# A hybrid RWKV/FNet/pooling trunk on one core: group matrices rebuilt in 64x64 quarters of the array, modulation products on four column strips

## The chip, the core and the metric

The kernel runs on one core of a Trainium2 chip. The metric is the device time of one execution in microseconds (us), as the median of several runs. The engines are TensorE (PE; its weight loads are listed as PEld), VectorE (DVE), ScalarE (ACT), GpSimd (POOL) and the DMA queues, of which SyncE (SP) issues most.

## What is computed

One layer of a trunk over 128 context tokens and 512 latent tokens of 1024 channels, all in float32:

```
shift1, scale1, gate1, shift2, scale2, gate2 = split(silu(cond) @ w_ada + b_ada)
h = rms_norm(x) * (1 + scale1) + shift1
proj = h @ w_in                        # columns for r, k, v, two low-rank inputs, FNet, pooling
y_a = rwkv_mixer(centred_shift(proj))  # 8 heads x 64, forward and backward
y_b = fourier_mixer(proj)              # y_c = pool_mixer(proj)
x = x + gate1 * (concat(y_a, y_b, y_c) @ w_out)
x = x + gate2 * (relu(h2 @ w_ff1)**2 @ w_ff2)      # h2 = modulated norm of x

# rwkv_mixer: decay and a come from low-rank products (w_up, a_up); then for each token
sa = S @ a;  S = S * w + sa b^T + v k^T;  y = S @ r
```

Outputs are the normed `x` of both token sets and the final state `S` of the context.

## The kernel before

**Products.** The large weights are split into two float32r parts (`whi`, `wlo`) and multiplied with the two parts of the activations, three products for each block: the tiles `hhi`/`hlo`, `mh`/`ml`, `h2h`/`h2l` and `fh`/`fl` are activations of w_in, w_out, w_ff1 and w_ff2. Small float32 products stand in the profile as two MATMUL records for each instruction, float16 ones and transposes as one.

**The mixer.** Time is cut into 10 chunks of 64 tokens; a head pair `j` (4 of them) and a direction `d` (2) have three groups of 2, 4 and 4 chunks, so there are 24 groups, 16 of four chunks and 8 of two. `prep` makes the elementwise operands of a group from two low-rank products (`wup` with `th`, `aup` with `adt`). `group` is a generator over stages, which yields after each: Gram blocks (`AR`,`BK`, result `EB`), the inverse of a triangular matrix of every chunk by doubling over five levels (`NB`, `X`, `XT`, `P1`) with one correction, the products W and Z, the matrices `OO`, and then a serial chain over the chunks that carries the state `x` (tiles `xr`) and adds to the output. Two 64-row blocks of a pair of chunks share the partitions. Before the change the operands `NB` and `XT` of the inverse (tiles `bda`) are block-diagonal, 128 x 128 with zero blocks; `oop` (tiles `oopa`) has zero blocks too; and `xr` has an identity in the half that the state doesn't use, so that one product with `OO` gives both terms.

**Order.** `run_groups` steps the generators of up to four groups while `Clock` estimates when each engine and tile is done. Where no group's next operands are there yet by that estimate, it steps the queue `gemms` (`in_rest`: the other w_in blocks; then the modulation of sections 2 to 5, `ada_steps`; then `out_half`: half of w_out), or, with that not ready, a dummy product on `lmask` whose result nobody reads. FNet, pooling and the transposes of x (`slow`), and `post` for each finished head pair (`y,bones`, `hsel,sq`, `ident,sq`, `kds,bones`, `sg,gup`) are stepped between. All engines issue in the order so traced.

**Modulation.** `ada_steps` multiplies the 32 columns of `sil` (two are used) with 512 columns of a 128-row block of `w_ada`; the four strips of 32 array columns belong to four row blocks, and in sections 2 to 5 each step brings one block.

After the mixer: the other half of w_out, the second norm, and the feed-forward product.

Of the kernel before, what the change touches and what calls it, by code (L numbers as in the profile page):

```python
# [13 lines left out]
F32 = mybir.dt.float32  # L14
# [146 lines left out]
class Clock:  # L161
    """estimate of when each engine and each tile is done with what has been traced; chooses what is traced next"""
# [7 lines left out]
    def __init__(self):  # L170
        self.free = dict.fromkeys("PVSGD", 0.0)
        self.done, self.used, self.slots = {}, {}, {}
        self.end = 0.0

    def cost(self, e, name, out, a, k):
        n = math.prod(out.shape[1:])
        if e == "P":
            if name == "transpose":
                return 55.0
            x = a[1]  # L180
            if x.dtype != F32:
                return n / 2.4 + (0.5 if x.dtype == F32R else 1.0)
            if out.shape[0] > 64:
                return max(211.0, n / 0.6 + 5.0)
            return 79.0 if n <= 64 else 133.0 * n / 128
# [10 lines left out]
    def tile(self, x):  # L196
        """name of the tile; a new one waits for the last use of the tile whose place it takes"""
# [12 lines left out]

    def note(self, e, name, out, a, k):
        rd = [self.tile(x) for x in list(a) + list(k.values()) if hasattr(x, "tensor")]
# [23 lines left out]
class Timed:  # L236
    """an engine whose instructions are noted on the clock"""
# [15 lines left out]
class Task:  # L253
# [4 lines left out]
    def step(self):  # L258
        """one step; it may yield the time that passes before the next, or the tile that the next reads first"""
# [11 lines left out]
def build(nc, tc, T):  # L271
# [10 lines left out]
    def pin(start):  # L282
        """the compute engines issue what was traced since start in the order of the program"""
# [35 lines left out]
    def wsplit(src, c0, hf, lo_eng, raw=None, to=None):  # L319
        """half of the rows of a block of 128 columns"""  # L320
# [9 lines left out]
    def gemm_steps(pss, w, a, kb, first, last, extra=0):  # L330
        """the products of one block of rows, as a generator over the matrix products"""
# [19 lines left out]
    def gemm(src, c0, a, lo_eng, halves=(0, 1), extra=0):  # L351
        """[P, NT] product with a block of 128 columns of the weights: two banks"""
# [32 lines left out]
    mod = cp.tile([P, 48, 2], F32, name="mod")  # L385

    def ada_steps(ks, slots, nk, ahead, queue=None):
        """sections of the modulation: 1024 columns each, 512 at a time; slots name the places of the weights"""
        todo = [(k, h, k2) for k in ks for h in range(2) for k2 in range(KB // nk)]
        place = {}  # L390

        def load(n):
            if queue is None and n < len(todo):
                k, h, k2 = todo[n]
                pool, tag, bufs = slots[n % len(slots)]
                place[n] = pool.tile([P, nk, 512], F32, tag=tag, name="wa", bufs=bufs)
                c0 = k * D + 512 * h
                dma(place[n][:], T["w_ada"][nk * k2 * P:nk * (k2 + 1) * P, c0:c0 + 512].rearrange("(a p) n -> p a n", p=P))

        for n in range(ahead):  # L400
            load(n)
        for n, (k, h, k2) in enumerate(todo):
            load(n + ahead)
            r = place.pop(n) if queue is None else queue.pop(0)
# [11 lines left out]
            yield  # L416
            ps2 = pm()
# [42 lines left out]
    XR = [[const(f"xr{d}{i}", [P, 2, C]) for i in range(3)] for d in range(2)]  # L460
# [24 lines left out]
    for d in range(2):  # L485
        for x in XR[d]:
            for q in range(2):
# [662 lines left out]
    def group(c, d, g, pool, own, pc, AR, BK):  # L1150
# [27 lines left out]
        if not M1:  # L1178
            yield
# [590 lines left out]
```

## Time and profile before

| | |
|---|---|
| median of 3 runs | 1140.12 us (1136.89 to 1140.99) |
| span of the profiled execution | 1140.2 us, which is its time |
| PE / PEld busy | 1095.3 us (96%) / 949.0 us (83%) |
| DVE / ACT / POOL busy | 544.5 / 506.4 / 383.3 us |
| mean granted TensorE clock | 0.983 of 2.4 GHz |

Busy PE is the union of the spans of pipelined products, so it doesn't tell how fast they follow each other. That is read from the start of a row of the timeline to the start of the next one, divided by the number of records in it.

### The profile page before, as it was taken

How to read it: one execution, taken by the hardware profiler on the slowest of the kernel's cores; microseconds unless marked ns; L12 is line 12 of the kernel's file. 1: busy time of each engine (PE TensorE's matmuls, PEld its weight loads, DVE VectorE, ACT ScalarE, POOL GpSimd, SP SyncE). 2: the span in 40 equal slices, each digit the busy share in tenths (PEclk: the TensorE clock that was granted, in tenths of full speed). 3: DMA queues.
4: the chain of work that ended last, by engine and by line, in shares of the span. 5: the costliest groups of instructions: out<-in, count | busy, mean ns of one | idle time of the engine just before them, and what ended most of it. 6: DMA issues, size and time to landing. Idle time of an engine off the chain costs nothing.

```text
span 1140.2 us, 23679 instructions
## 1 busy us (share of the span) xinstructions
PE 1095.3 (96%) x9516; PEld 949.0 (83%) x9516; DVE 544.5 (48%) x1297; ACT 506.4 (44%) x1221; POOL 383.3 (34%) x462
## 2 busy tenths in 40 slices
PE   5999999999999998998999999999999999999996
PEld 3688888788785665565677999999999999999996
DVE  6266665466665654667754664311331233123313
ACT  5243575655565454654762354312431243124412
POOL 4224431124222133464300283333333333333520
PEclk9999999999998999998999999999999999999999
DMA  9522311111313345442313322222222222222212
GB/s 321 184 62 81 94 36 58 51 51 43 95 64 121 112 139 166 124 133 69 111 56 97 117 74 75 75 75 75 75 76 80 76 76 75 75 74 75 77 45 93
DMA packets 130383, 104.11 MB, mean 91 GB/s; under 512 B 9309, under 2 KB 108642, under 8 KB 130274
## 3 DMA queue, kind: packets, MB, share of 16 engines
q1 hardware_dynamic: 114290, 81.22, 23.5%
q10 hardware_dynamic: 15552, 21.05, 6.2%
q8 instruction: 75, 1.23, 0.4%
q0 software_dynamic: 432, 0.33, 0.2%
q14 instruction: 34, 0.28, 0.1%
HBM read 90.52 MB, written 9.76 MB: 88 GB/s over the span
## 4 chain that ended last, share of the span: by engine, by line
PE 82%; issue 6%; DVE 6%; POOL 2%; ACT 1%; DMA 0%; ACTq 0%; DVEq 0%; POOLq 0%
PE pb L248 82%; DVE t L248 1%; DVE EB L248 1%; DVE bda L248 1%; POOL st L248 1%; DVE P L248 1%; DVE hlo L248 0%; DVE BK L248 0%; POOL t L248 0%; DMA wpl<-w_pool 0%; POOL bda L248 0%; ACTq L248 0%; DVE dd L248 0%; DVE W L248 0%; DVE y L248 0%
## 5 line engine op out<-in xcount | busy, mean ns | idle before, releaser
L248 POOL TENSOR_TENSOR wlo<-raw,whi 128x512 fp32r<-128x512 f32 x125 | 162.3, 1299 | 268.5 <-ACT whi L248 266.2
L248 ACT CAST whi<-raw 128x512 fp32r<-128x512 f32 x161 | 99.8, 620 | 276.6 <-PE pb L248 251.0
L248 PE MATMUL pb<-h2l,whi 128*128 128x320 f32 (+1 forms) x512 | 155.4, 310 | 0.0
L248 PE MATMUL pb<-h2h,whi 128*128 128x320 f32 (+1 forms) x512 | 155.3, 311 | 0.0
L248 DVE SCALAR_TENSOR_TENSOR x<-pb,mod,x 128x128 f32<-128x128 f32 (+1 forms) x144 | 55.0, 433 | 172.9 <-PE pb L248 172.7
L248 PE MATMUL pb<-fh,whi 128*128 128x320 f32 (+2 forms) x408 | 123.3, 310 | 0.0
L248 PE MATMUL pb<-fl,whi 128*128 128x320 f32 (+2 forms) x408 | 122.7, 308 | 0.0
L248 PE MATMUL pb<-h2h,wlo 128*128 128x320 f32 (+1 forms) x512 | 117.0, 310 | 0.0
L248 PE MATMUL pb<-hhi,whi 128*128 128x320 f32 (+1 forms) x304 | 99.1, 331 | 0.0
L248 PE MATMUL pb<-hlo,whi 128*128 128x320 f32 (+1 forms) x304 | 98.6, 329 | 0.4 <-DVE hlo L248 0.4
L248 PEld LDWEIGHTS pb<-h2l,whi 128*128 128x128 f32 x512 | 96.6, 189 | 0.0
L248 PEld LDWEIGHTS pb<-h2h,whi 128*128 128x128 f32 x512 | 96.5, 189 | 0.0
L248 PE MATMUL pb<-fh,wlo 128*128 128x320 f32 (+2 forms) x408 | 94.6, 309 | 0.0
L248 PEld LDWEIGHTS pb<-h2h,wlo 128*128 128x128 f32 x512 | 86.3, 188 | 0.0
L248 POOL TENSOR_TENSOR t<-t,k 128x256 f32<-128x256 f32 (+1 forms) x24 | 15.9, 664 | 208.2 <-DVE t L248 197.5
L248 PE MATMUL pb<-hhi,wlo 128*128 128x320 f32 (+1 forms) x304 | 78.8, 328 | 0.0
L248 PEld LDWEIGHTS pb<-fh,whi 128*128 128x128 f32 x408 | 77.1, 189 | 0.0
L248 PEld LDWEIGHTS pb<-fl,whi 128*128 128x128 f32 x408 | 76.3, 187 | 0.0
L248 DVE TENSOR_TENSOR rl<-pb,rs 128x320 f32<-128x320 f32 x64 | 30.3, 486 | 94.3 <-PE pb L248 94.1
L248 PEld LDWEIGHTS <-bda 128*128 128x128 f16 x880 | 43.1, 99 | 37.8 <-issue 13.9
L248 ACT COPY W<-pb 128x256 f32<-128x256 f32 (+3 forms) x144 | 54.4, 398 | 41.5 <-DVE W L248 29.2
L248 PEld LDWEIGHTS pb<-fh,wlo 128*128 128x128 f32 x408 | 68.6, 188 | 0.0
(271 smaller groups left out, 2399.7 us busy)
## 6 DMA issues: line engine op xcount, KB each, us to landing
raw<-w_ff SPq DMA_DIRECT2D x128, 256.0 KB, 2.8
wa<-w_ada SPq DMA_DIRECT2D x64, 256.0 KB, 3.2
wa<-w_ada SPq DMA_DIRECT2D x16, 512.0 KB, 8.7
raw<-w_in SPq DMA_DIRECT2D x30, 256.0 KB, 2.9
raw<-w_out SPq DMA_DIRECT2D x16, 256.0 KB, 2.8
ukd<-shq ACTq DMA_DIRECT2D x9, 320.0 KB, 2.5
ds<-dft_s ACTq DMA_DIRECT2D x8, 257.0 KB, 2.7
x<-x_sample SPq DMA_DIRECT2D x4, 512.0 KB, 5.8
```

Source lines behind the costliest of these rows:

```text
L248: return fn(out, *a, **k)
```

## The change

The operands with zero blocks go. The inverse is done with 64 x 64 products on the diagonal quarters of the array; `X` and `XT` share a tile `XX`, which leaves PSUM in one copy. The `OO` matrices come from 64 x 64 products `EB`,`WW` on all four quarters; the terms of Z and V go apart from them: `EB`,`ZV` gives `ZP`, which is added to the state in each chain step, and `ZV`,`EB` goes straight into the output bank. A chain step is one VectorE instruction on 128 partitions in place of one each on VectorE and ScalarE. The Gram products alternate between the two row halves. In `prep` the two low-rank products stand next to each other on opposite row halves (the two halves of the columns of that w_in block are swapped for it, so that its early load comes in two parts of 64 columns). `ada_quads` takes 128 columns of four row blocks in each step, on the four strips. The costs in `Clock` are new, among them one for every change of the shape of the array's tiles. Comments are removed as well.

```diff
--- before.py
+++ after.py
@@ class Clock
+            if x.dtype == F32R:
+                return n / 2.4 + 13.5
             if x.dtype != F32:
-                return n / 2.4 + (0.5 if x.dtype == F32R else 1.0)
-            if out.shape[0] > 64:
+                return n / 2.4 + 1.0 if x.shape[0] > 64 else 18.0
...
+    def mode(self, name, out, a):
+        m = (a[1].shape[0] > 64, out.shape[0] if name != "transpose" else P)
+        if m != self.was:
+            self.was = m
+            self.free["P"] += 95.0
@@ modulation
+    def ada_quads(ks, slots, ahead):
+        todo = [(k, h, cb, k2) for k in ks for h in range(2) for cb in range(4) for k2 in range(2)]
...
+                place[n] = pool.tile([P, 4, P], F32, tag=tag, name="wa", bufs=bufs)
...
+            for i in range(4):
+                q = 32 * i
+                mm(ps[q:q + 32, cb * P:(cb + 1) * P], sil[:, 4 * k2 + i, :], r[:, i, :], start=k2 == 0, stop=k2 == 1, tile_position=(0, q))
...
-        gemms.append(task(ada_steps((2, 4, 3, 5), [(wp, "whi", WB), (wp, "wlo", WB)], 1, AH)))
+        gemms.append(task(ada_quads((2, 4, 3, 5), [(wp, "whi", WB), (wp, "wlo", WB)], AH)))
@@ prep
-        ps = pm()
+        ps, ps2 = pm(), pm()
         mm(ps[:, 0:w], wup[rows, js], th[rows, cs], start=True, stop=True)
+        mm(ps2[:, 0:w], aup[HR[1 - d], js], adt[HR[1 - d], cs], start=True, stop=True)
...
-        mm(ps[:, 0:w], aup[rows, js], adt[rows, cs], start=True, stop=True)
@@ group: Gram blocks
+        pss = [pm(), pm()]
+        for l in range(n):
+            for h in range(2):
+                mm(pss[h][:, l * P:(l + 1) * P], BKc[HR[h], l * P:(l + 1) * P], AR[HR[h], :, l, :], start=True, stop=True)
@@ group: inverse
-            for u in range(U):
-                mm(ps[:, (o + u) * C:(o + u + 1) * C], lhs[:, u, :], rhs(u), start=True, stop=True)
+            for u, i, R in units():
+                mm(ps[R, (o + u) * C:(o + u + 1) * C], lhs[R, u, :], rhs(u, R), start=True, stop=True)
...
-            diag(XT, lambda u: p1[:, u, :])
-            for u, i, R in units():
-                mm(ps[R, (U + u) * C:(U + u + 1) * C], p1[R, u, :], XT[R, u, i * C:(i + 1) * C], start=True, stop=True)
+            diag(XT, lambda u, R: p1[R, u, :])
+            diag(p1, lambda u, R: XT[R, u, :], U)
...
-                cp(X[:, 0:U, :], v4(ps, C, U))
-                for i, R in enumerate(HR):
-                    cp(XT[R, 0:U, i * C:(i + 1) * C], ps[R, U * C:2 * U * C].rearrange("p (u b) -> p u b", b=C))
...
+                cp(XX[:, :, 0:U, :], both)
@@ group: O matrices
-        for h in range(2):
-            ps = pm()
-            for l in range(n):
-                mm(ps[:, l * P:(l + 1) * P], oop[:, l // 2, l % 2, h * P:(h + 1) * P], EB[:, h, l, C:3 * C], start=True, stop=True)
...
+        for l2 in range(n2):
+            for h in range(2):
+                for i in range(2):
+                    mm(pss[i][HR[h], l2 * P:(l2 + 1) * P], WW[HR[i], 2 * l2 + h, :], EB[HR[i], h, 2 * l2 + i, C:3 * C], start=True, stop=True)
...
+                mm(ps[HR[h], l * C:(l + 1) * C], EB[:, h, l, P:3 * C], ZV[:, l // 2, l % 2, h * C:(h + 1) * C], start=True, stop=True)
...
+        V.tensor_tensor(ZP[:, 0:n, :], v4(ps, C), pc[:, 0:n].unsqueeze(2).broadcast_to([P, n, C]), op=ALU.mult)
@@ group: chain
+                mm(psy[HR[h], l * C:(l + 1) * C], ZV[:, l // 2, l % 2, h * C:(h + 1) * C], EB[:, h, l, C:P], start=l == 0, stop=False)
...
-                    mm(ps[HR[q], 0:C], OO[:, q, l, C:P], x[:, q, :], start=True, stop=True)
+                    mm(ps[HR[q], 0:C], OO[HR[q], l, C:P], x[HR[q], :], start=True, stop=True)
...
-                V.tensor_scalar(xn[HR[0], 0, :], ps[HR[0], 0:C], pc[HR[0], l:l + 1], None, op0=ALU.mult)
-                S.activation(xn[HR[1], 1, :], ps[HR[1], 0:C], AF.Copy, scale=pc[HR[1], l:l + 1])
+                V.scalar_tensor_tensor(xn[:], ps[:, 0:C], pc[:, l:l + 1], ZP[:, l, :], op0=ALU.mult, op1=ALU.add)
```

What this makes of the program is seen in the order of the instructions, where `x8` is the number of equal ones in a row. PE in `prep` and the Gram blocks of an early group, before the change:

```order
L248 MATMUL pb<-th,wup 128x256
L248 MATMUL pb<-xr_109,W_1740 64x64 x2
L248 MATMUL pb<-W_1740,xr_109 64x64 x2
...
L248 MATMUL pb<-AR,BK 128x128 x8
L248 MATMUL pb<-adt,aup 128x256
L248 MATMUL pb<-ident,sq 128x128 x5
```

The two low-rank products stand apart, with a chain step and Gram products between. The same place after the change:

```order
L262 MATMUL pb<-hsel,sq 128x2 x4
L262 MATMUL pb<-th,wup 128x256
L262 MATMUL pb<-adt,aup 128x256
L262 MATMUL pb<-hsel,sq 128x2
L262 MATMUL pb<-EB,ZV 64x64 x4
L262 MATMUL pb<-xr_109,OO 64x64 x2
L262 MATMUL pb<-OO,xr_109 64x64 x2
```

The second low-rank product now follows the first at once; the chain step (`xr`,`OO`) has the same number of instructions.

PE at the end of the last group before the change, with its `OO` matrices (`EB`,`oopa`) and its first chain step; `mh`/`ml` with `whi`/`wlo` is `out_half`:

```order
L248 MATMUL pb<-W_8651 64x128 x8
L248 MATMUL pb<-mh,whi 128x320
...
L248 MATMUL pb<-ml,whi 128x320
L248 MATMUL pb<-EB,oopa_909 128x128 x8
L248 MATMUL pb<-mh,wlo 128x320 x2
...
L248 MATMUL pb<-xr_113,W_9114 64x64 x2
L248 MATMUL pb<-W_9114,xr_113 64x64 x2
```

And after the change, where `lmask` is the dummy:

```order
L262 MATMUL pb<-W_9437 64x128 x8
L262 MATMUL pb<-wa,sil 32x128 x4
...
L262 MATMUL pb<-EB,WW 64x128 x8
L262 MATMUL pb<-ZV,EB 64x64 x8
L262 MATMUL pb<-wa,sil 32x128 x4
L262 LDWEIGHTS lmask
L262 MATMUL pb<-lmask 128x512
...
L262 MATMUL pb<-EB,ZV 64x64 x8
L262 MATMUL pb<-xr_113,OO 64x64 x2
L262 MATMUL pb<-OO,xr_113 64x64 x2
```

Eight products of 128 x 128 became eight on quarters and two times eight on half the array's columns, and what stands between them is modulation (`wa`,`sil`) and dummies instead of w_out.

PE in `post` of the last head pair, before the change:

```order
L248 MATMUL pb<-y,bones 128x512
L248 MATMUL pb<-y,bones 128x128
L248 MATMUL pb<-ml,whi 128x320
L248 MATMUL pb<-mh,wlo 128x320 x2
L248 MATMUL pb<-hsel,sq 128x2
L248 MATMUL pb<-mh,whi 128x320
```

And after it:

```order
L262 MATMUL pb<-y,bones 128x512
L262 MATMUL pb<-y,bones 128x128
L262 MATMUL pb<-ident,xq 128x128 x8
L262 MATMUL pb<-mh,whi 128x320
L262 MATMUL pb<-hsel,sq 128x2
L262 MATMUL pb<-ml,whi 128x320
```

The first products of `out_half` stood far ahead of this place before the change; now the last transposes of x (`ident,xq`) and then the first of `out_half` are here. Of its 192 products, 111 stood ahead of the last `sg,gup` before, and 10 do now.

Counted over the whole program: the shape of PE's tiles (128 x 128, 64 x 64, 128 x 64, 64 x 128 or 128 x 32) changes 712 times before and 772 times after; dummies are 103 and 79; MATMUL instructions are 8093 and 9461. The 64 modulation steps of sections 2 to 5 stand in 36 places before and in 45 after (31 with one step, 10 with two, 3 with three, 1 with four).

## Rows read from the trace of the kernel before

**Rows 1.** Windows by stage: us, busy PE, PEld, DVE, ACT, POOL, PEclk, DMA share.

```profile
80.00:345.00 265.00, 261.77 (x2792) 217.04 (x2790) 168.63 (x423) 152.84 (x441) 77.69 (x136) 0.99 0.21 64
345.00:600.00 255.00, 237.87 (x2662) 159.27 (x2657) 155.56 (x405) 147.43 (x417) 84.56 (x122) 0.96 0.38 116
600.00:690.00 90.00, 86.46 (x623) 81.39 (x618) 51.59 (x106) 35.83 (x66) 35.65 (x25) 0.96 0.33 95
690.00:1140.20 450.20, 441.57 (x3009) 441.17 (x3007) 128.33 (x273) 140.36 (x237) 159.04 (x127) 1.00 0.25 74
```

**Rows 2.** Who PE waited for, 80 to 690 us: us, times, longest; 14 rows.

```profile
PE pb L248 <- DVE P L248: 4.2, 9, 1.5
...
PE pb L248 <- ACT y L248: 0.2, 1, 0.2
```

**Rows 3.** Timeline of PE (start, length us, records): inverse of a group.

```profile
136.99 0.22 PE L248 MATMUL pb<-X,bda 128*128 128x64 f16 x2
137.04 0.28 PE L248 MATMUL pb<-P,bda 128*128 128x64 f16 x4
137.25 0.31 PE L248 MATMUL pb<-bda,P 64*64 64x64 f16 x8
137.50 0.41 PE L248 MATMUL pb<-hhi,wlo 128*128 128x322 f32 x1
```

**Rows 4.** Timeline of PE: a modulation step of sections 2 to 5.

```profile
347.64 1.05 PE L248 MATMUL pb<-wa,sil 128*32 128x512 f32 x2
348.62 0.29 PE L248 MATMUL pb<-P,bda 128*128 128x64 f16 x4
```

**Rows 5.** Timeline of PE: products of 128 columns on four strips, first stage.

```profile
59.32 0.64 PE L248 MATMUL pb<-w,shp 128*32 128x128 f32 x16
59.89 0.41 PE L248 MATMUL pb<-hlo,whi 128*128 128x320 f32 x1
```

**Rows 6.** Timeline of PE: Gram products, four chunks and two.

```profile
160.67 1.71 PE L248 MATMUL pb<-AR,BK 64*128 64x128 f32 x16
...
228.47 0.72 PE L248 MATMUL pb<-AR,BK 64*128 64x128 f32 x8
```

**Rows 7.** Timeline of PE: the first of the two low-rank products.

```profile
139.43 0.70 PE L248 MATMUL pb<-th,wup 64*128 64x256 f32 x2
140.05 0.34 PE L248 MATMUL pb<-xr,W 128*64 128x64 f32 x4
```

**Rows 8.** Timeline of PE: O matrices of a group of four chunks.

```profile
609.57 1.95 PE L248 MATMUL pb<-EB,oopa 128*128 128x128 f32 x16
611.27 0.54 PE L248 MATMUL pb<-mh,wlo 128*128 128x320 f32 x2
```

**Rows 9.** Timeline of PE: five dummies and a chain step.

```profile
209.74 1.25 PE L248 MATMUL pb<-lmask 128*128 128x512 bf16 x5
210.92 0.34 PE L248 MATMUL pb<-xr,W 128*64 128x64 f32 x4
...
211.30 0.41 PE L248 MATMUL pb<-hhi,whi 128*128 128x320 f32 x1
```

**Rows 10.** Groups of ACT, 80 to 690 us: copies of the inverse, EB.

```profile
L248 ACT CAST bda<-pb 64x256 f16<-64x256 f32 x128 | 47.0, 368 | 1.0
L248 ACT CAST X<-pb 128x256 f16<-128x256 f32 x64 | 24.1, 377 | 16.6 <-PE pb L248 13.8 <-DMA oopa<-vt 1.8
L248 ACT COPY EB<-pb 128x512 f32<-128x512 f32 x16 | 9.4, 588 | 2.1 <-PE pb L248 1.7
```

**Rows 11.** Windows on both sides of a fall of PEclk.

```profile
273.00:276.40 3.40, 3.40 (x52) 2.99 (x50) 2.37 (x7) 1.79 (x6) 1.41 (x2) 1.00 0.04 12
276.40:279.80 3.40, 3.40 (x18) 3.34 (x19) 1.64 (x4) 2.61 (x10) 3.06 (x5) 0.50 0.05 10
```

**Rows 12.** Timeline of PE: post of the last head pair, its longest wait.

```profile
628.13 1.30 PE L248 MATMUL pb<-ident,sq 128*128 128x128 f32 x5 [1.94 <-DVE sq L248]
```

**Rows 13.** Who PE waited for, 0 to 80 us: modulation weights.

```profile
PE pb L248 <- DMA wa<-w_ada: 1.9, 2, 1.7
```

More of the change, by code (lines that the diff above doesn't have):

```diff
@@ L385, in build, with ada_steps @@
     mod = cp.tile([P, 48, 2], F32, name="mod")
-    def ada_steps(ks, slots, nk, ahead, queue=None):
+    def ada_steps(ks, nk, queue):
         todo = [(k, h, k2) for k in ks for h in range(2) for k2 in range(KB // nk)]
[L390 to L401, printed above, removed]
         for n, (k, h, k2) in enumerate(todo):
-            load(n + ahead)
-            r = place.pop(n) if queue is None else queue.pop(0)
+            r = queue.pop(0)
             yield r[:]
@@ L416, in ada_steps, with load @@
             yield
+            ps2 = pm()
+            for i in range(4):
+                PE.transpose(ps2[:, i * P:(i + 1) * P], asb[:, i * P:(i + 1) * P], ident[:])
+            ms = mod[:, 8 * k + 4 * h:8 * k + 4 * h + 4, :]
+            V.tensor_reduce(ms, ps2[:].rearrange("p (n q c) -> p n c q", n=4, q=4)[:, :, 0:2, :], axis=mybir.AxisListType.X, op=ALU.add)
+            V.tensor_tensor(ms, ms, pv("b_ada", 8 * k + 4 * h, 4).unsqueeze(2).broadcast_to([P, 4, 2]), op=ALU.add)
+            yield
+    def ada_quads(ks, slots, ahead):
+        todo = [(k, h, cb, k2) for k in ks for h in range(2) for cb in range(4) for k2 in range(2)]
+        place = {}
+        def load(n):
+            if n < len(todo):
+                k, h, cb, k2 = todo[n]
+                pool, tag, bufs = slots[n % len(slots)]
+                place[n] = pool.tile([P, 4, P], F32, tag=tag, name="wa", bufs=bufs)
+                c0 = k * D + 512 * h + P * cb
+                dma(place[n][:], T["w_ada"][4 * k2 * P:4 * (k2 + 1) * P, c0:c0 + P].rearrange("(a p) n -> p a n", p=P))
+        for n in range(ahead):
+            load(n)
+        for n, (k, h, cb, k2) in enumerate(todo):
+            load(n + ahead)
+            r = place.pop(n)
+            yield r[:]
+            if cb == 0 and k2 == 0:
+                ps = pm()
+            for i in range(4):
+                q = 32 * i
+                mm(ps[q:q + 32, cb * P:(cb + 1) * P], sil[:, 4 * k2 + i, :], r[:, i, :], start=k2 == 0, stop=k2 == 1, tile_position=(0, q))
+            if cb < 3 or k2 == 0:
+                continue
+            asb = wp.tile([P, 512], F32, tag="raw", name="asb", bufs=RB)
+            V.tensor_copy(asb[:], ps[:])
+            yield asb[:]
             ps2 = pm()
@@ L726, in wload @@
                 ws[b, hf] = wp.tile([P, 4, P], F32, tag="raw", name="raw", bufs=RB) if b >= NRAW else pq.tile([P, 4, P], F32, name=f"w{b}{hf}") if b < 3 else w3[:, hf]
-                dma(ws[b, hf][:], w_in[:, 4 * hf:4 * hf + 4, early[b][0]:early[b][0] + P])
+                c0 = early[b][0]
+                if c0 == AD_OFF:
+                    for q in range(2):
+                        dma(ws[b, hf][:, :, HR[q]], w_in[:, 4 * hf:4 * hf + 4, c0 + C * (1 - q):c0 + C * (2 - q)])
+                else:
+                    dma(ws[b, hf][:], w_in[:, 4 * hf:4 * hf + 4, c0:c0 + P])
             def load(n=4):
@@ L1292, in group @@
             x = nextx()
-            for q in range(2):
-                G.memset(x[HR[q], q, :], 0.0)
+            G.memset(x[:], 0.0)
             c[d]["x"] = x
```

132 lines of the change are left out of this document (62 added, 70 removed).

## The prediction

> **What bounds the kernel now.** I read the windows by stage first. From 690 us on the kernel runs w_out and the feed-forward, which the change leaves alone; from 80 to 690 us lie the 24 groups with the work stepped between them, and PE is busy there nearly throughout [rows 1]. The list of waits says the same from the other side: all that PE waited for between 80 and 690 us are 14 rows that sum to 23.3 us, the largest 4.2 us for DVE [rows 2]. So in this stage PE has a queue of work, and what counts is how much time its instructions take up, not how long one lasts. The timeline gives that, from the start of one row to the start of the next: 16 records of the O matrices take 611.27 - 609.57 = 1.70 us, 0.106 us each [rows 8]; five dummies with one change of tile shape behind them 1.18 us, some 0.215 us each and 0.10 us for the change [rows 9]. That change is the second thing to see. Two full products of the inverse take 0.05 us, so four take 0.11; but the four ahead of the quarter products need 0.21 until the next row, and these eight need 0.25 [rows 3]. Each change of tile shape thus costs about 0.10 us, and 712 of them some 70 us: of the size of the products themselves.
>
> **The change part by part, as PE time.** The counts are those of the section on the change, over the whole program.
>
> Modulation. One step, one instruction in two records, takes 0.98 us with its change of shape [rows 4]. Steps that stand together lie on different strips and run beside each other, so I count places: 36 x 0.98 = 35.3 us. The new step is four instructions of 128 columns on four strips. The first stage has just these with other operands: 16 records, two such steps, in 0.57 us with the change [rows 5], so with 0.215 us for a further step (two passes of 128 columns at the O matrices' 0.106) a lone one takes 0.36. 31 x 0.36 + 10 x 0.57 + 3 x 0.79 + 1.0 = 20.3 us. Saved: 15.0.
>
> Gram products. With one row half after the other 16 records last 1.71 us; where eight records of a two-chunk group ran with the halves beside each other they lasted 0.72 [rows 6]. Alternating, 16 should last 0.72 + 4 x 0.106 = 1.15: 0.55 us less in each of 16 groups, 8.8 us; the two-chunk groups I leave. Bound below: nothing, if the halves don't overlap.
>
> Low-rank products. One takes 0.62 us with its change [rows 7], 0.52 without. On opposite row halves the second lies under the first: 16 x 0.52 and, at half the columns, 8 x 0.3 make 10.7 us. Bound below: nothing.
>
> O matrices. 320 records at 0.106: 34 us [rows 8]. In their place, for a four-chunk group: 16 records on four quarters, four deep, 4 x 0.106 and some 0.1 to begin, 0.53 us; and twice 16 records of 64 columns on two column halves, of which eight take 0.38 us with a change [rows 9], so 16 some 0.51. 1.55 x 20 = 31, saved 3.0. The trace has no product on four quarters; if only two run at once, 0.43 x 20 = 8.6 us more, and the part loses 5.6. I take four, since four strips run at once [rows 5], and two diagonal quarters too [rows 3].
>
> Inverse. 880 full products, 220 blocks of four at 0.11 us, become 1,760 quarter products, 220 blocks of eight at 0.25 - 0.10 = 0.15 [rows 3]. A block that follows another without a change gives its tail away, so the loss lies between 0 and 220 x 0.04 = 8.8 us; I take 2.
>
> The chain has as many products as before. Dummies: 24 fewer, 24 x 0.215 = 5.2 us [rows 9]. Changes of shape: 60 more, 9 of them already in the modulation; 51 x 0.10 = 5.1 us lost.
>
> Sum: -15.0 - 8.8 - 10.7 - 3.0 + 2.0 - 5.2 + 5.1 = -35.6 us.
>
> **What it does to waits.** Less PE work means less cover for the steps on DVE and ACT, of which the inverse alone has eleven in each group. Against that, these steps get shorter. After each level ACT made three copies in a row, 0.377 + 2 x 0.368 = 1.11 us; now one of 512 columns, for which the copy of EB is the nearest row: 0.59 [rows 10]. DVE and ACT are busy at most 64% of a stage [rows 1], so even with 35 us out of it neither becomes the bound. I add 3 us to the 23.3, with bounds of -8 and +20: a third fewer, or nearly as many again.
>
> Two smaller places. The early w_in block that comes in two parts of 64 columns has half as long pieces; the modulation weights behind it are waited for 1.9 us now [rows 13]; I add 1 us, 0 to 2. At the end, 111 of 192 products of `out_half` stood ahead of the last `sg,gup` and now 10. This is no more work, but `post` of the last head pair then has little beside it: its longest wait, behind a norm on GpSimd and VectorE, is 1.94 us with such products in front [rows 12]. I add 3 us, 0 to 6. The products that come later cover the way of `y` through memory, so that is free; if they were missing it would show as a wait of w_out.
>
> **The forecast.** 1140.2 - 35.6 + 3 + 1 + 3 = 1111.6, **1112 us**. The sum is made against the profiled execution, which is 0.1 us from the median. A measurement of this kernel tells about 0.5% from no change, 5.7 us.
>
> **The rivals.** (B) PE stays as full and the shorter steps take waits away: -8 in place of +3, nothing at the start and the end, and the upper price of the inverse not met (0): 1140.2 - 37.6 - 8 = 1095. For it speaks that ACT loses about half of its copies in the inverse; against, that the waits are few already and most hang on DVE, whose steps stay as long.
>
> (C) The second half of the stage has no more work to fill in. From 345 us on `in_rest` is used up, PE is 93% busy against 99% before [rows 1], and what fills is modulation and dummies. If all that is saved there (the 15 us of modulation, and 120 of the 240 Gram and as large a share of the other products) turns into waits for the inverse of the last groups, only 8 to 10 us of the 36 stay: 1131. For it: between the products of the last group now stand single modulation steps of 0.36 us and dummies. Against: the dummies are fewer by count, so the order expects fewer gaps.
>
> (D) Slower: the granted clock. In the stage 345 to 600 us it is 0.96 [rows 1], and before one fall PE was busy the whole 3.4 us with 52 records, many on part of the array, and at 0.50 afterwards [rows 11]. More small tiles could mean more such falls. The clocks of the three stages [rows 1] amount to 5 + 20 + 7 = 32 us at 1.2 GHz between 80 and 690 us, costing at most half of it. The forecast gains 28.6 us; to lose 5.7 as well, PE would have to spend some 69 us more at 1.2 GHz, three times what it does now in all. 1146 us or more. Against it: fewer dummies and fewer full products are a small part of the stage, and `in_rest` and w_out stay as they are.
>
> (E) The change doesn't do what it says: tiles don't run beside each other in the new places. No gain of Gram and low-rank products and two quarters at a time: 8.8 + 10.7 + 8.6 = 28 us, 1140. The Trainium skill has a rule that would do it in another place, in TensorEngine Tiling (Array Packing), Gotcha 1: PSUM Pressure: different row tiles must not use one PSUM bank at once. The quarter products of the inverse of both row halves write to one bank; by that rule each block of eight would take eight times 0.029 us in place of 0.15, and 220 blocks some 18 us more. The quarter products of before speak against that [rows 3]: eight such products, on both row halves and into one bank, took 0.25 us with their change, too little for one after the other. The new Gram and O products use a bank for each row half.
>
> **Chances.** The forecast (own range 1101 to 1123) 0.61; B 0.12; C 0.17; D 0.05; E 0.05. The bounds of the inverse, the four quarters and the waits reach 20 us to either side of 1112, so the range is **1094 to 1132**: it holds the forecast, half of B and two thirds of C. Faster by over 0.5% (under 1134.4) are the forecast, B and most of C: 0.88. Within 0.5% the rest of C and half of E: 0.06. Slower: D and a little of E: 0.06.
>
> **What would show it.** In the profile after: 16 Gram records in about 1.15 us; the two low-rank products in one row of some 0.6 us; `EB`,`WW` x16 with the next row about 0.55 us behind (0.95 if two at a time); a lone step of the modulation in 0.36 us; changes of shape still near 0.10 us; the windows from the last group on as long as before; and waits of PE that sum to about 26 us between 80 us and the end of `post`. The prediction is wrong if these waits double, if PEclk falls below 0.9 in the second half of the groups, or if the stage before 345 us gains as little as C allows.

## The result

The changed kernel takes 1145.32 us (median of 7 runs, 1143.09 to 1149.16) against 1137.9 us before (7 runs, 1136.89 to 1141.69): a ratio of 1.0054, 95% interval 1.0031 to 1.0078. It is slower by half a per cent; 1112 us was forecast, and the range ended at 1132. The profiled execution has a span of 1141.3 us and a mean granted clock of 0.967, against 1140.2 and 0.983. A span is 1.8 us less than the time of its run (1143.09 us for this one), so the profiled execution of before is one of its longer ones and that of after its shortest: they differ by 1.1 us, the medians by 7.

The windows by stage of the kernel after, with the columns of [rows 1]:

```profile
80.00:345.00 265.00, 252.20 (x3378) 193.28 (x3378) 145.61 (x396) 104.46 (x274) 58.65 (x104) 0.94 0.18 53
345.00:600.00 255.00, 227.80 (x3975) 170.82 (x3979) 161.73 (x440) 103.62 (x274) 91.64 (x136) 0.93 0.43 123
600.00:690.00 90.00, 84.78 (x580) 81.31 (x577) 47.69 (x97) 34.25 (x59) 32.57 (x24) 0.96 0.37 110
690.00:1141.20 451.20, 442.77 (x3017) 442.37 (x3015) 129.16 (x276) 141.03 (x239) 160.06 (x127) 1.00 0.25 74
```

PE is less busy in both stages of the groups (252.2 us where [rows 1] has 261.8, and 227.8 where it has 237.9), so work did go. But the clock is 0.94 and 0.93 where it was 0.99 and 0.96. The windows are equally long in both tables, and the stage behind them takes 451.2 us after 450.2: the groups end no earlier, with less work in them and more idle time of PE. Of the 21 us of idle time that came between 80 and 690 us, 9.6 lie ahead of 345 us. The list of waits of PE in the kernel after, 80 to 690 us (us in total, times, longest), beside [rows 2]:

```profile
PE pb L262 <- POOL xr L262: 11.9, 5, 4.7
PE pb L262 <- ACT XX L262: 9.5, 6, 4.1
PE pb L262 <- ACT W L262: 3.2, 1, 3.2
PE pb L262 <- DVE xr L262: 3.1, 2, 1.6
...
PE pb L262 <- issue: 0.3, 2, 0.2
```

These are 17 rows that sum to 43.4 us, against 23.3. The first two are places where PE waits for an engine's queue rather than for an engine's work.

The first: a chain that begins at zero begins with a memset of its state on GpSimd, and GpSimd takes its instructions in turn. The timelines of GpSimd and of PE in the kernel after, at one of the five places:

```profile
134.02 1.99 POOL L262 TENSOR_TENSOR st<-st,halfm 128x10 f32<-128x10 f32 x1 [9.31 <-DVE st L262]
135.96 0.15 POOL L262 MEMSET xr<- 128x64 f32 x1
```
```profile
136.17 0.48 PE L262 MATMUL pb<-xr,OO 64*64 64x64 f32 x4 [3.15 <-POOL xr L262]
```

A memset of 0.15 us stood behind the inverse root of a norm in `post` (`st`,`halfm`), which itself waited for DVE, and PE stood still for 3.15 us. The second: the one copy per level of the inverse is on ACT, and ACT also issues loads. Timelines of ACT (ACTq is its DMA issue) and PE in the kernel after:

```profile
403.15 0.33 ACTq L262 DMA_DIRECT2D k<-ukd  x1
...
404.06 1.08 ACTq L262 DMA_DIRECT2D v<-ukd  x1
405.19 0.93 ACTq L262 DMA_DIRECT2D s<-state  x2
...
407.41 0.39 ACTq L262 DMA_DIRECT2D wfn<-w_fnet  x1
407.90 0.58 ACT L262 CAST XX<-pb 128x512 f16<-128x512 f32 x1 [3.96 <-DMA s<-state]
```
```profile
408.54 0.31 PE L262 MATMUL pb<-XX,NB 64*64 64x64 f16 x8 [2.81 <-ACT XX L262]
```

And the products themselves? Timeline of PE in the kernel after (start, length, records), to be read from start to start as in [rows 3]:

```profile
131.62 0.48 PE L262 MATMUL pb<-th,wup 64*128 64x256 f32 x1
131.62 0.48 PE L262 MATMUL pb<-adt,aup 64*128 64x256 f32 x1
...
132.25 0.38 PE L262 MATMUL pb<-hsel,sq 128*128 128x2 f32 x2
...
403.99 1.16 PE L262 MATMUL pb<-AR,BK 64*128 64x128 f32 x16
405.08 0.65 PE L262 MATMUL pb<-W 64*64 64x128 f32 x8
...
468.00 0.29 PE L262 MATMUL pb<-P,XX 64*64 64x64 f16 x8
468.12 0.29 PE L262 MATMUL pb<-XX,P 64*64 64x64 f16 x8
468.35 0.71 PE L262 MATMUL pb<-AR,BK 64*128 64x128 f32 x8
...
596.87 0.67 PE L262 MATMUL pb<-EB,WW 64*64 64x128 f32 x16
597.46 0.69 PE L262 MATMUL pb<-ZV,EB 128*64 128x64 f32 x16
598.08 0.42 PE L262 MATMUL pb<-wa,sil 128*32 128x128 f32 x8
598.44 0.82 PE L262 MATMUL pb<-lmask 128*128 128x512 bf16 x3
599.19 0.69 PE L262 MATMUL pb<-EB,ZV 128*64 128x64 f32 x16
```

They cost what was forecast, or nearly: both low-rank products 0.63 us (some 0.6), 16 Gram records 1.09 (1.15), `EB`,`WW` 0.59 (0.55; four quarters do run at once), `ZV`,`EB` 0.62 with its change (0.51 and 0.10), a lone step of the modulation 0.36 (0.36), three dummies and a change 0.75 (0.215 each and 0.10).

### The profile page after: what moved, and what is told of

It is laid out like the page before. It is cut to its first block, busy times and chain, and to the rows that moved or that the text cites. A ratio compares the mean times of both kernels' runs of the same rounds, so it can differ in the third digit from the quotient of the medians.

```text
span 1141.3 us, 27113 instructions
## 1 busy us (share of the span) xinstructions
PE 1076.2 (94%) x11391; PEld 938.7 (82%) x11396; DVE 523.4 (46%) x1301; ACT 413.9 (36%) x909; POOL 366.0 (32%) x433
## 4 chain that ended last, share of the span: by engine, by line
PE 54%; issue 3%; DVE 3%; POOL 2%; DMA 1%; ACT 1%; ACTq 0%; DVEq 0%; POOLq 0%
PE pb L262 54%; POOL st L262 1%; ACTq L262 0%; DVE P L262 0%; POOL ra L262 0%; DMA px<-fpd 0%; DVE t L262 0%; DVE NB L262 0%; DVE EB L262 0%; DMA wfn<-w_fnet 0%; DMA wa<-w_ada 0%; DMA ZV<-vt 0%; DVE BK L262 0%; DVE y L262 0%; ACT t L262 0%
## 5 line engine op out<-in xcount | busy, mean ns | idle before, releaser
L262 PE MATMUL pb<-hhi,whi 128*128 128x320 f32 (+1 forms) x304 | 103.4, 344 | 0.0
L262 PE MATMUL pb<-hlo,whi 128*128 128x320 f32 (+1 forms) x304 | 102.9, 343 | 0.1
L262 PE MATMUL pb<-hhi,wlo 128*128 128x320 f32 (+1 forms) x304 | 84.5, 338 | 0.1
L262 ACT CAST XX<-pb 128x512 f16<-128x512 f32 (+1 forms) x96 | 49.1, 517 | 96.8 <-PE pb L262 69.3
L262 PEld LDWEIGHTS pb<-hlo,whi 128*128 128x128 f32 x304 | 57.9, 190 | 10.5 <-issue 5.6
```

The source lines that it names most:

```text
L262: return fn(out, *a, **k)
```

## The experiments

**Theory W** says that the work was saved and came back as waits of PE behind the queues of GpSimd and ACT, and as the falls of the clock that start in these waits. **Theory C**: the clock falls because products on parts of the array count for less, waits or not. **Theory S**: the order that the estimate wrote is poor as a whole, so that the waits are that order's. The three ask for different edits.

In the table, "waits" are the rows of PE's list of waits from 80 to 690 us, added up, and "slow" is the time at 1.2 GHz, 2 x span x (1 - mean clock). "Sum" is what should follow against the profile of the kernel named: the work on PE that the edit adds (changes of shape at 0.10 us, dummies at 0.215, steps of the modulation as in the forecast), the difference of the waits, and half of the difference of the slow time. "Spans" is what the profiled executions differ by.

| run | ratio to before (95%) | span | clock | waits | slow | sum | spans |
|---|---|---|---|---|---|---|---|
| before | 1 | 1140.2 | 0.983 | 23.3 | 38.8 | | |
| after, against before | 1.0054 (1.0031 to 1.0078) | 1141.3 | 0.967 | 43.4 | 75.3 | -35.6+20.1+18.3 = +2.8 | +1.1 |
| e1, against after | 0.9973 (0.9945 to 1.0001) | 1132.7 | 0.970 | 35.8 | 68.0 | -7.6-3.7 = -11.3 | -8.6 |
| e2, after | 0.9966 (0.9945 to 0.9987) | 1139.5 | 0.964 | 36.1 | 82.0 | -7.3+3.4 = -3.9 | -1.8 |
| e3, after | 0.9997 (0.9978 to 1.0016) | 1134.8 | 0.980 | 32.0 | 45.4 | 14.6-11.4-15.0 = -11.8 | -6.5 |
| e4, after | 0.9865 (0.9837 to 0.9892) | 1125.4 | 0.977 | 34.3 | 51.8 | -9.1-11.8 = -20.9 | -15.9 |
| e5, before | 0.9988 (0.9969 to 1.0006) | 1143.0 | 0.978 | 22.1 | 50.3 | -1.2+5.8 = +4.6 | +2.8 |
| e6, before | 0.9987 (0.9970 to 1.0004) | 1141.8 | 0.973 | 32.4 | 61.7 | -16.3+9.1+11.5 = +4.3 | +1.6 |
| e7, after | 0.9930 (0.9902 to 0.9958) | 1131.2 | 0.963 | 42.8 | 83.7 | -11.9-0.6+4.2 = -8.3 | -10.1 |
| e8, before | 1.0278 (1.0254 to 1.0303) | 1173.5 | 0.972 | 29.0 | 65.7 | 7.8+5.7+13.5 = +27.0 | +33.3 |
| e9, e4 | 0.9942 (0.9920 to 0.9963) | 1137.1 | 0.980 | 27.4 | 45.5 | 23.8-6.9-3.2 = +13.7 | +11.7 |
| e10, after | 0.9838 (0.9808 to 0.9869) | 1120.9 | 0.971 | 39.4 | 65.0 | -11.9-4.0-5.2 = -21.1 | -20.4 |
| e11, after | 0.9905 (0.9872 to 0.9937) | 1125.6 | 0.977 | 35.6 | 51.8 | 4.0-7.8-11.8 = -15.6 | -15.7 |
| e12, after | 1.0020 (0.9992 to 1.0049) | 1146.3 | 0.964 | 45.1 | 82.5 | 0.9+1.7+3.6 = +6.2 | +5.0 |
| e13, after | 0.9800 (0.9774 to 0.9826) | 1112.8 | 0.981 | 28.1 | 42.3 | 4.0-15.3-16.5 = -27.8 | -28.5 |
| e14, before | 1.0069 (1.0044 to 1.0094) | 1147.1 | 0.983 | 26.4 | 39.0 | -1.3+3.1+0.1 = +1.9 | +6.9 |
| e15, before | 1.0218 (1.0179 to 1.0257) | 1166.2 | 0.972 | 36.8 | 65.3 | 6.3+13.5+13.3 = +33.1 | +26.0 |
| e16, after | 0.9933 (0.9902 to 0.9964) | 1128.5 | 0.978 | 43.4 | 49.7 | -0.1+0-12.8 = -12.9 | -12.8 |
| e17, after | 1.0029 (1.0006 to 1.0052) | 1140.8 | 0.971 | 42.3 | 66.2 | 3.6-1.1-4.6 = -2.1 | -0.5 |
| e18, after | 1.0063 (1.0033 to 1.0094) | 1140.4 | 0.970 | 41.9 | 68.4 | 3.6-1.5-3.5 = -1.4 | -0.9 |

The sums miss the spans by 2.7 us at most in 14 rows, and by 5.0 to 7.1 us in the other five (e3, e4, e8, e14, e15). So work on PE, waits and half of the slow time account for the larger differences; one of some 5 us can't be read from a single row. The question is then where the waits and the slow time come from.

A profile is one execution of many, and the slow time differs between executions of one kernel. In the ten runs of e12 the spans lie 13.8 us apart; less half of their slow time they lie 4.4 us apart. Over the runs whose span is on record before has a median of 29.6 us of slow time (96 runs, 13.6 to 55.0) and after one of 80.0 (7 runs, 73.0 to 89.5). So the clock costs the change some 25 us by the medians, more than the 18 of the profiled pair. Less half of the slow time the medians of the spans are 1122.4 and 1103.3 us: work and waits together gave 19 us back, and the clock took more than that. The profiled executions of e2, e5, e6, e8, e9, e14 and e15 are the longest of their kernels.

### The queues: e1, e2, e4, e5

In e1 a constant tile `xz` takes the place of the state that is zeroed; the estimate still counts the memset, so every engine keeps its order.

```diff
         if g == 0:
             x = nextx()
-            G.memset(x[:], 0.0)
-            c[d]["x"] = x
...
+            c[d]["x"] = xz
```

> Kernel after, but the groups that begin a chain at zero read one tile that is zeroed once, in place of a state tile that GpSimd zeroes just ahead of the chain; every engine keeps the order of its other instructions. Theory W (what the change saved on PE came back as PE's waits behind full queues of GpSimd and ACT, and the clock falls that start in these waits): the five waits for that memset (11.9 us of PE) go, some short ones come in their place, and the falls that begin at 133, 246 and 516 us (three times 6.8 us at 1.2 GHz) go too: 8 to 18 us shorter than after, 1127 to 1137 us, and PE's time at 1.2 GHz between 80 and 690 us falls from 72 to about 50 us. Theory C (the clock falls because products on parts of the array count for less, waits or not): the waits go, but the time at 1.2 GHz stays near 72 us: 4 to 9 us shorter. Theory S (the order is poor as a whole, so a wait taken away only comes back a little later for another engine): less than 3 us.

Measured: 8.6 us off the span, the waits for `POOL xr` gone, 7.6 us less of waits and 7 us less of slow time. It is at the low end of theory W and at the high end of what C allows, so it doesn't part these two; theory S's bound of 3 us falls. Some of the wait came back: `DVE sq` grew from 2.8 to 6.0 us. The three falls of the clock that were to go did not go: two came half as long (shown below), the third as long as before, behind a wait of 2.9 us for `DVE sq`.

In e2 loads that ACT issued go to SyncE, again in an unchanged order:

```diff
+    def adma(out, src):
+        clock.note("A", "dma_start", out, (src,), {})
+        return nc.sync.dma_start(out, src)
...
-        S.dma_start(dftc[:], T["dft_c"])
+        adma(dftc[:], T["dft_c"])
```

> Kernel after, but 47 loads (of the next head pair, of FNet, pooling and the transposes of x) are issued by SyncE in place of ACT; the order of everything else stays. Theory W: PE's waits for ACT's copies at 408, 476 and 562 us (2.8, 4.1 and 3.2 us, behind runs of four to nine such issues) go, with the falls of the clock at 410 and 475 us and part of that at 564: 8 to 18 us shorter than after. Theory S: less than 3 us, since the same groups wait for something else next. If SyncE, which also issues the weights and waits for their places, becomes late instead, waits for weights appear and it is longer.

Measured by the medians, 1135.34 us, some 10 us off kernel after; the profiled execution is one of the longer ones and shows 1.8 us. The waits for `ACT XX` fell from 9.5 to 3.2 us and the one for `ACT W` went, and one new wait of 3.5 us for a weight of the modulation came, as the last sentence of the expectation said it might. The slow time did not fall in this execution (82.0 us); the median of the twelve runs is 72.5 us, against 80.0 for after.

> The edits of the first two kernels together: no memset ahead of a chain, and the 47 loads on SyncE. Theory W: both gains add, 18 to 32 us shorter than after, 1113 to 1127 us, which is also faster than before by 1 to 2 per cent; PE waits between 80 and 690 us for about 23 us, as before the change, and is at 1.2 GHz for about 35 us. Theory S: 5 us or less.

Measured: 1124.1 us, a ratio of 0.9865: the two gains add, and the kernel is faster than before. That the waits would be back at 23 us and the slow time at 35 was too much: they are 34.3 and, over the whole span, 51.8.

> Kernel before, with the same 47 loads issued by SyncE in place of ACT; the order of everything else stays. If the change made PE sensitive to full queues (theory W), before gains less than the 10 us that after did: it waits 3.8 us for a copy of ACT at 446 us with a fall of the clock, so 2 to 6 us shorter. If the loads are a cost that both kernels have alike, 8 to 11 us shorter, and then they explain nothing of the difference.

Measured: 0.9988, not clear of 1: less than either case, the 2 to 6 us of theory W included. The wait of 3.8 us at 446 us went and a wait of 4.8 us for a weight of the modulation came. So the loads are not a cost that both kernels have alike.

### The clock: e3, e17, e18

In e3 there is more work and nothing else:

```diff
                 ps = pm()
+                if g == 0 and ii == 0:
+                    for _ in range(8):
+                        nc.tensor.matmul(ps[:, 0:512], lm2[:, 0:P], lm2[:, 0:512], start=True, stop=True)
                 for q in range(2):
```

> Kernel after, with eight more dummies of 128 x 512 (0.215 us each, 1.72 us) right ahead of the first chain step of each of the eight groups that begin at zero; nothing else moves. Five of these places wait now for 3.15, 1.65, 1.79, 4.67 and 0.63 us, three not at all. By waits alone the dummies cost 0.07 + 1.09 + 3 x 1.72 = 6.3 us, and some 0.1 us for each change of shape: +7 us. Theory C: that, +7 us, with the falls of the clock where they are. Theory W: the falls at 133, 246 and 516 us do not come, or later, since PE works through the waits; they cost up to half of 20 us: between -4 and +3 us, and about 20 us less at 1.2 GHz.

Measured: 64 more dummies, 13.8 us of work, and the kernel is not 7 us longer but 6 us shorter than after, more than the 4 that theory W allowed. Windows of the kernel after, and of e3, around the wait for the memset shown above:

```profile
130.00:133.50 3.50, 2.87 (x26) 2.10 (x24) 1.01 (x5) 1.89 (x4) 0.00 (x0) 1.00 0.43 152
133.50:140.30 6.80, 4.13 (x51) 3.79 (x52) 2.41 (x8) 1.27 (x4) 5.02 (x8) 0.51 0.02 4
```
```profile
130.00:133.50 3.50, 3.33 (x29) 2.40 (x28) 1.01 (x5) 1.90 (x4) 0.00 (x0) 1.00 0.46 160
133.50:140.30 6.80, 5.32 (x89) 3.76 (x87) 3.71 (x10) 1.66 (x6) 5.13 (x8) 1.00 0.00 1
```

With the wait filled by dummies the fall does not come, and 89 records are done in the window where 51 were. The small products are all still there, so they alone do not bring the clock down at this place. But the dummies do two things at once: they fill the wait, and they put products on the full array among the small ones. e1 parts these two, since it takes the wait away and adds no work. Its windows at the place where after waits 1.65 us for a memset at 246 us:

```profile
241.00:244.40 3.40, 3.40 (x48) 2.70 (x44) 1.90 (x9) 1.27 (x3) 0.51 (x1) 1.00 0.00 0
244.40:247.80 3.40, 3.40 (x19) 2.60 (x20) 1.84 (x5) 1.35 (x3) 1.48 (x1) 0.50 0.00 0
247.80:251.20 3.40, 3.40 (x29) 2.46 (x29) 3.37 (x7) 0.72 (x2) 1.51 (x3) 1.00 0.26 77
```

PE is busy without a gap and the clock falls all the same, for 3.4 us in place of the 6.8 of after. At 135.2 us, behind waits of only 0.40 and 0.63 us, it is the same: 3.4 us in place of 6.8. The fall of before at 276.4 us [rows 11] has no wait ahead of it either. So falls of both kinds exist. Each of the ten falls of after between 80 and 690 us has a wait of 1.45 to 4.7 us just ahead of it, as theory W says; and small products without a wait can have one too, as theory C says. At the two places here, taking the wait away halved the fall, and filling it with products on the full array prevented it.

One stretch at 1.2 GHz didn't fit theory W either: it lasts 13.6 us, although PE is busy throughout. e17 and e18 put eight dummies ahead of the wait at its start and one chain step behind it:

```diff
+                if g == 1 and j == 0 and ii == 0:      # e17; in e18 ii == 1
+                    for _ in range(8):
+                        nc.tensor.matmul(ps[:, 0:512], lm2[:, 0:P], lm2[:, 0:512], start=True, stop=True)
```

> Kernel after with eight dummies (1.72 us) ahead of the first chain step of the two groups of head pair 0 that start from the given state; one of these places is the wait of 1.45 us at 172.7 to 174.2 us, where the clock falls for 13.6 us. Theory W (the wait starts the fall): no fall at 174 us, the stretch is at 2.4 GHz and some 6 us shorter, and the whole 2 to 6 us shorter than after in spite of 1.9 us more work at the other place. Theory C (small products bring the clock down wherever they stand): the fall comes there or within some us, and the time is that of after or 2 us more.

> The same dummies one chain step later, at about 176 us, behind the wait and inside the stretch at 1.2 GHz. If the clock stays low because the work there is products on parts of the array (what is left of theory C): the stretch ends some 3 to 7 us earlier, and the time stays within 3 us of after although 16 dummies are added. If it has a length of its own once it has fallen: 13.6 us as before, plus 3.4 us for eight dummies at half the clock, and 4 to 6 us longer than after.

The same stretch in the kernel after, in e17 and in e18:

```profile
171.00:174.40 3.40, 1.95 (x41) 1.46 (x38) 2.82 (x7) 0.99 (x3) 0.03 (x1) 1.00 0.00 0
174.40:188.00 13.60, 13.60 (x133) 9.90 (x130) 4.90 (x15) 2.68 (x6) 2.03 (x6) 0.50 0.07 20
```
```profile
174.40:188.00 13.60, 13.60 (x201) 9.52 (x201) 7.23 (x26) 5.78 (x14) 2.13 (x6) 1.00 0.07 20
```
```profile
174.40:188.00 13.60, 12.77 (x149) 8.24 (x149) 5.77 (x18) 4.22 (x11) 2.10 (x6) 0.87 0.07 20
```

In e17 there is no fall, and 201 records are done in place of 133. In e18 the wait is still there and so is the fall, but it lasts 2 x 13.6 x 0.13 = 3.5 us. So here the fall does not come when the wait is filled with work on the full array, and the work behind the wait decides how long it lasts: chain steps and quarter products with single blocks of w_in between them kept the clock at 1.2 GHz for 13.6 us, and eight products on the full array among them ended it. That much more of theory C holds. That this wait alone starts the fall is not shown, since no run takes it away without adding work. The time of the whole kernel hardly moved (1.0029 and 1.0063), since other falls came (one of 3.4 us at 348 us in e17, with PE busy ahead of it) and 16 dummies were added.

### The work that was saved: e6, e9

e6 is the kernel before with the new `ada_quads` alone, which the old costs price like the old steps, so that nothing else moves.

> Kernel before with the new modulation alone (128 columns of four row blocks on the four strips); the estimate gives it the same cost, so the order of all other work is that of before, with four instructions where one stood. The prediction has 15 us less work of PE for it, all after 345 us. If that reaches the end: 13 to 17 us shorter than before, 1121 to 1126 us. By theory W the places where these steps stand fill gaps, and what they no longer cover turns up as PE's waits (20.3 us between 345 and 690 us before) and time at 1.2 GHz: 3 to 9 us shorter, with waits of 25 to 32 us in that stretch.

Measured: 0.9987, not clear of 1. Less than either theory had: some 16 us of work went from PE and nothing came out at the end. The timeline and the first rows of the waits in e6:

```profile
348.77 0.42 PE L248 MATMUL pb<-wa,sil 128*32 128x128 f32 x8
349.29 0.28 PE L248 MATMUL pb<-P,bda 128*128 128x64 f16 x4
```
```profile
PE pb L248 <- ACT oopa L248: 7.3, 2, 6.9
PE pb L248 <- DVE P L248: 4.6, 9, 1.5
PE pb L248 <- issue: 3.2, 1, 3.2
```

A step and its change now take 0.52 us, 0.10 of it idle, where [rows 4] has 0.98. PE arrives 1.8 us earlier at the same copy of ACT, and the copy, behind eight issues of loads as before, is done 1.3 us later; so PE waits 6.9 us for it in place of 3.8. The waits rose by 9.1 us and the slow time by 23 (by the medians of the runs, 51.2 against 29.6, by 22).

e9 is the reverse swap in e4, one product of 512 columns again in each step:

```diff
-                mm(ps[q:q + 32, cb * P:(cb + 1) * P], sil[:, 4 * k2 + i, :], r[:, i, :], start=k2 == 0, stop=k2 == 1, tile_position=(0, q))
...
+            kb = 2 * cb + k2
+            q = 32 * (kb % 4)
+            nc.tensor.matmul(ps[q:q + 32, :], sil[:, kb, :], r[:].rearrange("p a n -> p (a n)"), start=kb < 4, stop=kb >= 4, tile_position=(0, q))
```

> The kernel with both edits (no memset ahead of a chain, 47 loads on SyncE), but each step of the modulation in sections 2 to 5 is again one product of 512 columns of one row block; nothing else moves in the order. If the new modulation is worth its work on PE once these queues are free: 14 to 20 us longer than the kernel with both edits (1138 to 1144 us). Theory W (this work stands in gaps that other waits, or the slower clock, fill when it is gone, as in kernel before, where the same swap brought 0.1 per cent): 0 to 8 us longer, 1124 to 1132 us, with fewer waits of PE behind 345 us.

Measured: 1133.82 us, 9.7 more than e4: between the two expectations. With the queues clear, some 40% of the 24 us of work reaches the end.

### The order: e7, e8, e10 to e16

e7 is the kernel after with the class `Clock` of before, e8 the kernel before with that of after; the products stay.

> Kernel after with the costs of before in the estimate that writes the order (no price for a change of shape): the same products in another order, with 694 changes of shape in place of 772 and 60 dummies in place of 79. Theory S (the new costs write a poorer order): faster than after by more than the 12 us that the changes and dummies amount to (78 x 0.10 + 19 x 0.215). Theory W: fewer dummies and less work, so more waits of PE and more time at 1.2 GHz; at most 8 us faster than after, or slower.

> Kernel before with the new costs: the same products as before, 756 changes of shape in place of 712 and 119 dummies in place of 103, so some 44 x 0.10 + 16 x 0.215 = 8 us more work of PE. Theory S: 10 us or more longer than before. Theory W: the dummies stand where the estimate sees a gap, and take the place of waits: 0 to 8 us longer.

Measured: e7 1132.72 us (0.9930), so 1.2% better than after, 14 us where its smaller count of changes and dummies is 12: just past theory S's bound, and past the 8 us of theory W. Its waits (42.8 us) and its slow time are no better than after's. e8 1171.69 us (1.0278): 32 us longer, of which counts explain 8. Theory S was right for e8.

> The kernel with both edits, and the costs of before in the estimate that writes the order. The two gains are of different places, if theory S holds for the order and theory W for the queues: the old costs took 1.2 per cent off kernel after and the two edits 1.9 per cent, so 1108 to 1116 us. If they are the same waits, taken away in two ways: 1120 to 1127 us, no faster than the edits alone.

Measured: 1122.44 us, in the second case (1120 to 1127): with intervals 0.6% wide it is not told from e4, so the old costs add nothing clear once the queues are free.

e11 and e12 nudge one cost:

```diff
-            self.free["P"] += 95.0
+            self.free["P"] += 85.0      # e11; in e12 105.0
```

> Kernel after with 85 in place of 95 as the price of a change of shape in the estimate: the same products in a slightly different order (803 changes of shape for 772, 83 dummies for 79, some 4 us more work of PE). If the waits behind full queues are a matter of this one order (theory S), the time moves by 8 us or more either way beside the 4. If they belong to the change (theory W), it stays within 4 us of after plus those 4, with 35 to 50 us of waits between 80 and 690 us.

> The same with 105 in place of 95 (777 changes of shape, 81 dummies, 1 us more work of PE). Theory S: 8 us or more to either side of after. Theory W: within 5 us of after, with 35 to 50 us of waits of PE between 80 and 690 us and some 60 to 80 us at 1.2 GHz.

Measured: 1127.49 us with 85 and 1140.44 with 105, for 1145.32 with 95. The first is theory S's: 18 us for a nudge that says nothing new of the chip. The second, 5 us, is within theory W's bound; its profiled execution is one of its longer ones, so its row in the table has the other sign.

> The two edits (no memset ahead of a chain, 47 loads on SyncE) with the price 85, whose order has a wait of 4.6 us for ACT's copies and 4.4 us for GpSimd's memset. If the edits take these waits and their falls of the clock (theory W): 8 to 14 us shorter than with 85 alone, 1113 to 1120 us. If the order with 85 had already got what the edits give (theory S): 1123 to 1129 us.

Measured: 1116.58 us, 0.9800 (0.9774 to 0.9826): the edits of the queues bring 11 us here too. It is the fastest of all.

The last three change `RD`, the slack that the estimate adds to every step, from 90.

> Kernel before, where the estimate adds 95 in place of 90 ns to each step; the same products in another order (714 changes of shape for 712, 96 dummies for 103). If the order of before is one of many alike: within 5 us of before. If it is a lucky one, chosen for these products: 8 to 25 us longer, with more than 35 us of waits of PE between 80 and 690 us or more than 55 us at 1.2 GHz.

> The same with 85 (721 changes of shape, 128 dummies, some 6 us more work of PE). Alike: within 5 us of before plus up to 6. Lucky order: 12 us or more longer than before.

> Kernel after with the same slack of 95 (762 changes of shape for 772, 83 dummies for 79). Orders of after so far: 1145, 1140 and 1127 us. Theory W alone (waits belong to the change): within 5 us of after. Theory S: anywhere between 1120 and 1145 us, in step with waits plus half of the time at 1.2 GHz.

Measured: before with 95 is 1146.65 us (1.0069) and with 85 1164.68 (1.0218); after with 95 is 1131.59 (0.9933). e14, 7.5 us longer, lies between its two cases, and with 26.4 us of waits and 39.0 of slow time it has neither sign of the second; e15 is clearly in the lucky one. e16 is theory S's: its waits add up to what after has, 43.4 us, it has 25.6 us less of slow time, and its span is 12.8 us shorter, which is half of that. That it fits to the tenth is luck, since other rows miss by several us.

## Why the prediction was wrong

**The work on PE** was right, as far as the rows show. The terms read above came within 0.06 us for each block; -35.6 us, with the waits and the slow time as measured, makes +2.8 where the spans differ by +1.1. The Trainium skill, TensorEngine Tiling (Array Packing), Gotcha 1: PSUM Pressure, says that different row tiles cannot access one PSUM bank at the same time; rival E weighed that. It did not show: at 468.00 us eight quarter products on both row halves into one bank took 0.12 us, where four products of 64 columns on the full array, one after the other, take 0.11 by [rows 3].

**The step that failed is "What it does to waits", and its number is "I add 3 us to the 23.3".** The waits between 80 and 690 us grew by 20.1 us, the upper bound of that sentence. The reason given for a small value, that neither DVE nor ACT becomes the bound by its busy share, was beside the point: none did. What PE came to wait for was an instruction of 0.15 us in GpSimd's queue and copies of ACT behind loads. The loads ahead of ACT's copies stood there before as well (the wait of 3.8 us). That the PE work which was removed had covered such waits is shown by e6 for the modulation alone, in an unchanged order; for the memsets and the other products it is argued, since the order changed with them.

**The clock was left out of the sum**, and rival D was priced as if it came alone: "some 69 us more at 1.2 GHz" to be slower. It was 36.5 us more (75.3 - 38.8) in the profiled executions and some 50 by the medians of the runs, and with 20.1 us of waits that was enough, since the two come together: filling a wait with full products took its fall away (e3, e17), taking the wait away halved it (e1). Rival C, the waits, and rival D, the clock, were one case and got two chances, 0.17 and 0.05, and neither was allowed to add to the other. D's mechanism, small tiles making falls, is there: small products keep the clock down after a wait (e18), and at 244.4 us in e1 they bring it down without one, as at 276.4 us in before [rows 11], which the prediction had read itself. What D lacked is that waits among them make these falls more and longer.

**Behind both lies a step that was never put down as one:** the 23.3 us of waits were taken as the kernel's, to which a change adds. They belong to one order. Three other orders of the kernel before (e14, e15, e8) are 0.7, 2.2 and 2.8% longer than the one that was profiled. Five orders of the changed kernel (after, e7, e11, e12, e16) run from 0.9905 to 1.0054, 0.9968 in the mean, against 1.0141 for the four of before: 0.0173 x 1139 = 20 us in favour of the change, in the direction and near the size of the 28.6 us that were forecast. Some 5 us of the 20 are the counts of dummies and changes of shape, which differ between these orders ("work" in the sums of the table). That mean is over a handful of nudges, and not a law; but the change was set against the best of the four orders seen of before, in the worst of the five seen of after.

Of the rest: the forecast set a span beside times ("0.1 us from the median"), which are 1.8 us apart, too little to matter. The wait in `post` (1.94 to 2.82 us for `sq`) and the early w_in block stayed within their bounds, and w_out and the feed-forward take as long as before. The shorter chain step shows no gain of its own, as forecast. Not settled is why those five orders differ as they do; no rule for a good one came out, only its measure (waits plus half of the slow time). With it stays open how much of the 20.1 us of waits belongs to the change and how much to this one order.

## What to carry to other kernels

Work taken out of a full engine is worth its time only as far as nothing was hidden under it: look, for each gap that it filled, at what stands in the queues of the other engines there, tiny instructions and DMA issues too, and clear these first (here a constant in place of a memset and loads on another queue turned a loss of 0.5% into a gain of 1.35%, and 2.0% with a luckier order). Where a planner writes the order, compare a change over a few nudged orders on both sides, since here a nudge alone moved the time by up to 2%. Price a wait of PE with half of the slow time that follows it, and look for that time behind small products without a wait too.

## What the chip showed that was not expected

Adding 64 dummies (13.8 us of work) made the kernel 6 us shorter (e3). After a wait of 1.45 us PE ran at 1.2 GHz for 13.6 us while it was busy without a gap, with small products and single blocks of w_in; eight products on the full array cut this to 3.5 us (e18). At 244.4 us in e1 the clock fell for 3.4 us although PE had been busy without a gap. DMA issues on ACT hold its other work up: eight of them from 403.15 to 407.8 us, 0.3 to 1.1 us a row.
